# First SwiGLU block: the third of the seven products moved ahead of the second, and the first step of the down projection moved in front of the fourth

## The chip, the cores and the metric

The kernel runs on one core of a Trainium2 chip. The metric is the device time of one execution in microseconds (us). A core has engines that each run their own instructions in order and wait for one another through semaphores: TensorE (PE, with its weight loads shown as PEld), VectorE (DVE), ScalarE (ACT), GpSimd (POOL) and SyncE (SP), which here issues most of the DMA transfers.

## The reference

One decoder layer over 512 tokens of width 1024, in float32. What matters here is its first block, a SwiGLU with a hidden width of 2816 = 22 x 128:

```python
def swiglu(x, w_gate, w_up, w_down):
    return (jax.nn.silu(x @ w_gate) * (x @ w_up)) @ w_down

x = x + 0.5 * swiglu(rms_norm(x, g_ffn1[l]), w_ffn1_gate[l], w_ffn1_up[l], w_ffn1_down[l])
...
x = x + 0.5 * swiglu(rms_norm(x, g_ffn2[l]), w_ffn2_gate[l], w_ffn2_up[l], w_ffn2_down[l])
```

Between the two SwiGLU blocks stand attention over a window, a convolution, attention over a memory, and their output projection; the change does not touch them.

## The kernel before

**Precision.** Every float32 operand of a large product is split into a high and a low part (`whi`, `wlo` for weights; `bh`, `bl` and `hh`, `hl` for activations), and three matmuls (high x high, low x high, high x low) stand for one. ACT makes the high part (L167, a cast), DVE the low part (L168, a subtraction).

**One SwiGLU.** `ffn` goes through the 22 blocks f of 128 hidden columns. Blocks 0 to 3 multiply directly. Blocks 4 to 21 (`fast`, L448) use seven products of half size in place of eight (Strassen's scheme, with the sums of the activations made once by `blocks` and the sums of the weights made for each f by `make_sums`, four additions on DVE, L126 to L129). A product is 12 matmuls of 128x256 (`product`, L439: four slices of the contraction, three matmuls each). In the order of the code before, with the weights that they take, the products are:

| in the code | weights | block of the activations | written to |
|---|---|---|---|
| first | w0, first half (gate) | B_11 | bank `b` |
| second | w0, second half (gate) | B_21 | bank `de`, left half |
| third | w1, first half (sum s12) | B_Q1 | bank `de`, right half |
| fourth | w1, second half (s12) | B_Q2 | bank `b`, added |
| fifth | w2, first half (sum s43) | B_22 | bank `de`, right half, added |
| sixth | w3 (the `vhi`, `vlo` pair) | B_T4 | bank `c` |
| seventh | w2, second half (s43) | B_T3 | bank `b`, added |

After the third product ACT copies the right half of `de` (L459), after the first it copies `b` (L455), after the fourth `b` again (L461). DVE adds `de` and the copies (L464), ACT takes the Silu (L465), and after the sixth and seventh products DVE and ACT finish the hidden block (L475, L479, L402, L403).

**Down projection.** `ROUNDS` cuts the 22 hidden blocks into six rounds. As soon as a round's hidden blocks are there, pieces of its down projection run between later blocks: `steps(f)` gives them, and for f from 8 to 21 there is one piece (`mid`) in each block, two steps `step(j)` of 24 matmuls (in blocks 20 and 21 four of 12), whose sums DVE adds to x (L506). The first step of the piece stands behind the fifth product, the others behind the seventh. A piece has one pair of split weights, d.

**Weights.** `Weights` holds a list of loads (DMAs of 512 KB into four buffers `wraw`) and a list of items, each of which is split into one of four pairs of buffers `whi`, `wlo` in turn, or into the single pair `vhi`, `vlo`. `next()` hands out the item that is next in the list and has the one three places on split (`conv_ahead=3`), so that the order of the items in `add_pair` (L108) has to be that of the calls of `next()` in `fast`, and both decide where the splits stand in the queues of ACT and DVE. Each buffer is free again when the last matmul on what it held is done. The written order is not quite that of the engines: a scheduler of the framework sets it when the program is built, from the dependencies between tiles.

The flag `memory` of `ffn_weights` is true for the first SwiGLU alone, the flag `last` of `ffn` for the second alone. Both SwiGLU blocks run the same `fast` before the change.

Of the kernel before, what the change touches and what calls it, by code (L numbers as in the profile page):

```python
# [34 lines left out]
AF = mybir.ActivationFunctionType  # L35
ALU = mybir.AluOpType
# [49 lines left out]
class Weights:  # L86
# [121 lines left out]
def layer(tc, ctx, a):  # L208
# [185 lines left out]
    def ffn(pool, norm, first, gain, hooks, next_gain, last):  # L394
# [53 lines left out]
        def fast(f, mid):  # L448
# [4 lines left out]
            w0 = W.next()  # L453
            product(b, w0, 0, B_11, True)
            ACT.copy(s12[:, l], b)  # L455
            product(de[:, l], w0, 512, B_21, True)
            w1 = W.next()
            product(de[:, r], w1, 0, B_Q1, True)
            ACT.activation(s45[:, r], de[:, r], AF.Copy, scale=-1.0)  # L459
            product(b, w1, 512, B_Q2, False)  # L460
            ACT.copy(s12[:, r], b)  # L461
            w2 = W.next()
            product(de[:, r], w2, 0, B_22, False)
            DVE.tensor_tensor(g, de, s12, op=ALU.add)  # L464
            ACT.activation(g, g, AF.Silu)  # L465
            rest = []
            for d in mid:
                rest += down(*d)
            if rest:
                rest.pop(0)()  # L470
            w3 = W.next()
            product(c, w3, 0, B_T4, True)
            ACT.copy(s45[:, l], c)
# [759 lines left out]
```

## Time and profile before

| | |
|---|---|
| time, median of three runs | 865.73 us |
| the three runs | 869.84, 865.34, 865.73 us |
| the profiled execution: its time | 870.17 us |
| the profiled execution: its span, first to last instruction | 868.1 us |
| PE busy | 861.3 us (99%) in 6361 matmuls |
| DVE busy | 698.3 us (80%) |
| ACT busy | 446.0 us (51%) |
| transfers | 91.45 MB, 105 GB/s on average |

The page of the profile gives the busy time of each engine over the whole span; its views by window give the same for stretches, a timeline gives each instruction's start and duration, and the view of waits says which engine stood still for which. The first SwiGLU's blocks 4 to 21 lie between about 70 and 340 us of the span, the second's between about 590 and 840 us. A matmul's modelled end lies behind the start of the next, so a busy PE is not PE at its densest: the distance from one start to the next has to be read from the timeline or from counts in windows.

### The profile page before, as it was taken

The numbers are of one execution on the slowest core, as the hardware profiler recorded it, in microseconds if no ns is written. First come the engines' busy times: TensorE is split into PE (matmuls) and PEld (weight loads), VectorE is DVE, ScalarE is ACT, GpSimd is POOL, SyncE is SP. The second block draws the span as 40 slices with busy tenths as digits, with TensorE's granted clock in tenths as the row PEclk, the third lists the DMA queues.
The fourth block names the chain that finished last, engine by engine and source line by source line (L and its number), as shares of the span: only waits on it lengthen the run. The fifth ranks groups of instructions, "written<-read, shape, count | busy, mean of one in ns | idle before, by whom it ended". The sixth has DMA issues, their size and how long they took to land.

```text
span 868.1 us, 15720 instructions
## 1 busy us (share of the span) xinstructions
PE 861.3 (99%) x6361; PEld 795.1 (92%) x6361; DVE 698.3 (80%) x1163; ACT 446.0 (51%) x740; POOL 27.9 (3%) x30
## 2 busy tenths in 40 slices
PE   9999999999999999999999999999999999999998
PEld 5889999999999999988776878889999999999998
DVE  7998877777868887869989976997987878787772
ACT  7455545455554454632939754454554444545440
POOL 0010000000000000300000021010000000000000
PEclk9999999999999999999999999999999999999999
DMA  7326334334454344232020333336333333333312
GB/s 271 122 83 165 94 97 122 99 110 134 111 145 146 97 113 130 95 97 62 0 62 13 110 89 84 99 90 159 105 106 121 95 121 85 116 98 99 121 49 99
DMA packets 34809, 91.45 MB, mean 105 GB/s; under 512 B 3248, under 2 KB 5808, under 8 KB 34736
## 3 DMA queue, kind: packets, MB, share of 16 engines
q1 hardware_dynamic: 32000, 85.99, 32.1%
q0 software_dynamic: 1584, 2.88, 2.1%
q10 hardware_dynamic: 1152, 1.57, 0.7%
q8 instruction: 50, 0.82, 0.4%
q14 instruction: 23, 0.19, 0.1%
HBM read 85.45 MB, written 2.10 MB: 101 GB/s over the span
## 4 chain that ended last, share of the span: by engine, by line
PE 92%; DVE 3%; ACT 2%; issue 1%; DMA 1%; SPq 0%; ACTq 0%; DVEq 0%
PE mm L347 15%; PE mm L348 14%; PE mm L349 14%; PE mm L444 11%; PE mm L446 11%; PE mm L445 11%; PE sc L444 2%; PE sc L446 2%; PE sc L445 2%; PE sc L347 1%; PE sc L349 1%; PE sc L348 1%; PE tp L948 1%; PE tp L962 1%; ACT p L913 1%
## 5 line engine op out<-in xcount | busy, mean ns | idle before, releaser
L444 PE MATMUL mm<-bh,whi 128*128 128x256 f32 x864 | 239.9, 278 | 0.2 <-ACT kept L459 0.2
L446 PE MATMUL mm<-bh,wlo 128*128 128x256 f32 x864 | 239.6, 277 | 0.0
L445 PE MATMUL mm<-bl,whi 128*128 128x256 f32 x864 | 239.6, 277 | 0.0
L348 PE MATMUL mm<-hl,whi 128*128 128x256 f32 (+1 forms) x640 | 184.7, 289 | 0.0
L349 PE MATMUL mm<-hh,wlo 128*128 128x256 f32 (+1 forms) x640 | 184.6, 289 | 0.0
L347 PE MATMUL mm<-hh,whi 128*128 128x256 f32 (+1 forms) x640 | 184.1, 289 | 0.0
L167 ACT CAST whi<-wraw 128x1024 fp32r<-128x1024 f32 (+2 forms) x122 | 124.1, 1021 | 106.2 <-PE mm L348 45.0
L168 DVE TENSOR_TENSOR wlo<-wraw,whi 128x1024 fp32r<-128x1024 f32 (+2 forms) x122 | 145.4, 1193 | 34.4 <-ACT whi L167 34.0
L446 PEld LDWEIGHTS mm<-bh,wlo 128*128 128x128 f32 x864 | 163.1, 189 | 0.0
L444 PEld LDWEIGHTS mm<-bh,whi 128*128 128x128 f32 x864 | 162.2, 188 | 0.5 <-ACT kept L459 0.4
L445 PEld LDWEIGHTS mm<-bl,whi 128*128 128x128 f32 x864 | 162.2, 188 | 0.2
L349 PEld LDWEIGHTS mm<-hh,wlo 128*128 128x128 f32 x640 | 120.8, 189 | 2.9
L347 PEld LDWEIGHTS mm<-hh,whi 128*128 128x128 f32 x640 | 120.1, 188 | 2.7
L348 PEld LDWEIGHTS mm<-hl,whi 128*128 128x128 f32 x640 | 120.1, 188 | 2.7
L168 DVE TENSOR_TENSOR wlo<-s,whi 128x1024 fp32r<-128x1024 f32 x72 | 87.9, 1222 | 36.0 <-ACT whi L167 35.6
L167 ACT CAST whi<-s 128x1024 fp32r<-128x1024 f32 x72 | 75.5, 1050 | 47.3 <-PE mm L445 43.5
L348 PE MATMUL mm<-xl,whi 128*128 128x512 f32 x192 | 75.9, 395 | 0.6 <-DVE xl L359 0.5
L347 PE MATMUL mm<-xh,whi 128*128 128x512 f32 x192 | 76.3, 402 | 0.0
L349 PE MATMUL mm<-xh,wlo 128*128 128x512 f32 x192 | 75.8, 395 | 0.0
L506 DVE SCALAR_TENSOR_TENSOR x<-mm,x 128x512 f32<-128x512 f32 x80 | 54.0, 682 | 3.7 <-PE mm L349 3.7
L167 ACT CAST vhi<-wraw 128x512 fp32r<-128x512 f32 x36 | 22.4, 622 | 62.7 <-PE sc L445 48.5
L126 DVE TENSOR_TENSOR s<-wraw 128x512 f32<-128x512 f32 x36 | 24.9, 691 | 32.6 <-DMA wraw<-in_wgu 32.6
(243 smaller groups left out, 1368.3 us busy)
## 6 DMA issues: line engine op xcount, KB each, us to landing
wraw<-in_wgu SPq DMA_DIRECT2D x86, 512.0 KB, 3.6
wraw<-in_wd SPq DMA_DIRECT2D x44, 512.0 KB, 3.7
wraw<-in_win SPq DMA_DIRECT2D x12, 512.0 KB, 3.5
x<-t POOLq DMA_DIRECT2D x8, 256.0 KB, 6.1
out<-t SPq DMA_DIRECT2D x7, 256.0 KB, 2.0
x<-in_xT SPq DMA_DIRECT2D x3, 512.0 KB, 6.6
wraw<-in_wout_a SPq DMA_DIRECT2D x6, 256.0 KB, 2.7
wraw<-in_wgu SPq DMA_DIRECT2D x4, 256.0 KB, 4.9
```

The source lines that it names most:

```text
L126: nc.vector.tensor_tensor(s12[:, l], u[:, l], u[:, r], op=ALU.add)
L167: nc.scalar.copy(hi[:, :cols], raw[:, :cols])
L168: nc.vector.tensor_tensor(lo[:, :cols], raw[:, :cols], hi[:, :cols].bitcast(F32), op=ALU.subtract)
L347: PE.matmul(ps[:, t], wh[:, w], hi(k)[:, t], start=one, stop=False, skip_group_check=cut > 1)
L348: PE.matmul(ps[:, t], wh[:, w], lo(k)[:, t], start=False, stop=False, skip_group_check=cut > 1)
L349: PE.matmul(ps[:, t], wl[:, w], hi(k)[:, t], start=False, stop=end, skip_group_check=cut > 1)
L444: PE.matmul(ps, wh[:, c], bh[k][:, block], start=one, stop=False, skip_group_check=not first)
L445: PE.matmul(ps, wh[:, c], bl[k][:, block], start=False, stop=False, skip_group_check=not first)
L446: PE.matmul(ps, wl[:, c], bh[k][:, block], start=False, stop=end, skip_group_check=not first)
L506: DVE.scalar_tensor_tensor(o, ps, 0.5, xd, op0=ALU.mult, op1=ALU.add)
L913: ACT.activation(self.p[n, h][:, c], src[h][:, i, c], AF.Exp, scale=self.fac[:, m : m + 1], bias=self.neg[:, m : m + 1], accum_out=self.de ...
L948: PE.transpose(ps[:, i * P : (i + 1) * P], self.p[n, h][:, c : c + P], ident)
```

## The change

In the first SwiGLU alone (`last` false, `memory` true), blocks 4 to 21 take their products in another order, and the list of weights follows:

- the third product (w1, B_Q1, right half of `de`) and ACT's copy of it stand ahead of the second (w0, B_21, left half of `de`), which now adds to a bank that the third has started (`first` is False);
- the first step of the down projection stands ahead of the fourth product, where it stood behind the fifth;
- in `add_pair` the item of the down weights d stands ahead of that of the sum s43.

```diff
-    def add_pair(self, gate, up, mid):
+    def add_pair(self, gate, up, mid, early):
...
         self.items.append((i + 1, 1024, 128, lambda: self.sums[i][0]))
+        if early:
+            for ap in mid:
+                self.add(ap, 128)
         self.items.append((i + 1, 1024, 128, lambda: self.sums[i][1]))
-        for ap in mid:
-            self.add(ap, 128)
+        if not early:
+            for ap in mid:
+                self.add(ap, 128)
...
-                W.add_pair(flat(gu[f, 0]), flat(gu[f, 1]), [down(*d) for d in mid])
+                W.add_pair(flat(gu[f, 0]), flat(gu[f, 1]), [down(*d) for d in mid], memory)
...
+            else:
+                w0 = W.next()
+                product(b, w0, 0, B_11, True)
+                ACT.copy(s12[:, l], b)
+                w1 = W.next()
+                product(de[:, r], w1, 0, B_Q1, True)
+                ACT.activation(s45[:, r], de[:, r], AF.Copy, scale=-1.0)
+                product(de[:, l], w0, 512, B_21, False)
+                rest = []
+                for d in mid:
+                    rest += down(*d)
+                if rest:
+                    rest.pop(0)()
+                product(b, w1, 512, B_Q2, False)
+                ACT.copy(s12[:, r], b)
+                w2 = W.next()
+                product(de[:, r], w2, 0, B_22, False)
+                DVE.tensor_tensor(g, de, s12, op=ALU.add)
+                ACT.activation(g, g, AF.Silu)
```

The lines that are left out before the `else` are the old order under `if last:`. Lines of the changed kernel have other numbers: L459 is L483 there, L168 is L173, L506 is L531, L347 to L349 are L352 to L354, L444 to L446 are L449 to L451.

**PE, block 9, before.** In these rows mm_134 is bank `de` of block 9, mm_133 its bank `b`, whi34 and wlo34 are w1 (s12), whi35 and wlo35 are w2 (s43); a bracket names the engines whose semaphores the instruction waits for. The last row of the third product is followed by the fourth:

```order
L446 MATMUL mm_134_1420<-bh_68_551,wlo34_1327 128x256
L444 MATMUL mm_133_1419<-bh_41_331,whi34_1326 128x256 [waits Activation_49]
L445 MATMUL mm_133_1419<-bl_42_332,whi34_1326 128x256
L446 MATMUL mm_133_1419<-bh_41_331,wlo34_1327 128x256
L444 MATMUL mm_133_1419<-bh_52_389,whi34_1326 128x256
```

Twelve rows on, the fifth product is the first to write bank mm_134 again, and it waits for ACT's copy of the third:

```order
L445 MATMUL mm_133_1419<-bl_69_552,whi34_1326 128x256
L446 MATMUL mm_133_1419<-bh_68_551,wlo34_1327 128x256
L444 MATMUL mm_134_1420<-bh_41_331,whi35_1358 128x256 [waits Activation_49]
L445 MATMUL mm_134_1420<-bl_42_332,whi35_1358 128x256
L446 MATMUL mm_134_1420<-bh_41_331,wlo35_1359 128x256 [waits DVE_49]
```

**PE, block 9, now.** The same place in the changed program, again from the last row of the product with s12; mm_140 is the bank of the down step, whi35 and wlo35 are now its weights d, and whi33 is the gate's w0:

```order
L451 MATMUL mm_134_1422<-bh_68_551,wlo34_1339 128x256
L352 MATMUL mm_140_1480<-hh_91_809,whi35_1358 128x256 [waits DVE_49,Activation_49]
L353 MATMUL mm_140_1480<-hl_92_810,whi35_1358 128x256
L354 MATMUL mm_140_1480<-hh_91_809,wlo35_1359 128x256 [waits DVE_49]
L352 MATMUL mm_140_1480<-hh_101_956,whi35_1358 128x256
L449 MATMUL mm_134_1422<-bh_41_331,whi33_1287 128x256 [waits Activation_49]
L450 MATMUL mm_134_1422<-bl_42_332,whi33_1287 128x256
```

The scheduler has put four matmuls of the down step directly behind the product with s12, and the product that the code names next, B_21 into the left half of the same bank, waits for an instruction of ACT: it is the copy of the right half (L483). The rest of the step follows behind B_21. All of blocks 8 to 21 read so.

**PE, block 6, now.** Blocks 4 to 7 have no down step in that place. Here mm_105 is `de`, mm_104 is `b`, whi21 is w1 and whi20 is w0:

```order
L451 MATMUL mm_105_975<-bh_68_551,wlo21_906 128x256
L449 MATMUL mm_104_974<-bh_41_331,whi21_905 128x256 [waits Activation_49]
L450 MATMUL mm_104_974<-bl_42_332,whi21_905 128x256
L451 MATMUL mm_104_974<-bh_41_331,wlo21_906 128x256
L449 MATMUL mm_104_974<-bh_52_389,whi21_905 128x256
L449 MATMUL mm_105_975<-bh_41_331,whi20_866 128x256 [waits Activation_49]
```

Four matmuls of the product B_Q2 stand there in their stead, and blocks 4 and 7 read the same; in block 5 it is three matmuls of a down step with 512 columns.

**DVE, from block 8 into block 9, before.** wlo35 is the low part of s43 for block 9, wlo36 that of the down weights d, L126 to L129 are the sums for the block after, and mm_129 and mm_132 are the two down steps of block 8:

```order
L126 TENSOR_TENSOR s12_26_1507<-wraw27_1330 128x512 [waits DMAHW4_49]
L129 TENSOR_TENSOR s43_26_1508<-wraw26_1304,wraw27_1330 128x512 [waits DMAHW3_49,DVE_49]
L127 TENSOR_TENSOR s12_26_1507<-wraw26_1304,s12_26_1507 128x512 [waits DVE_49]
L506 SCALAR_TENSOR_TENSOR x_69<-mm_129_1332,x_69 128x512 [waits PE_49]
L128 TENSOR_TENSOR s43_26_1508<-wraw26_1304,s12_26_1507 128x512 [waits DVE_49]
L168 TENSOR_TENSOR vlo37_1458<-wraw24_1181,vhi37_1457 128x512 [waits PE_49,Activation_49]
L475 TENSOR_TENSOR t_128_1238<-kept_126_1236,mm_122_1232 128x512 [waits PE_49,Activation_49]
L479 TENSOR_TENSOR t_128_1238<-t_128_1238,t_127_1237 128x512 [waits DVE_49]
L168 TENSOR_TENSOR wlo35_1359<-s43_23_1321,whi35_1358 128x1024 [waits Activation_49]
L403 TENSOR_TENSOR hl_131_1390<-t_128_1238,hh_130_1389 128x512 [waits Activation_49]
L506 SCALAR_TENSOR_TENSOR x_69<-mm_132_1393,x_69 128x512 [waits PE_49]
L168 TENSOR_TENSOR wlo36_1427<-wraw25_1243,whi36_1426 128x1024 [waits DMAHW2_49,Activation_49]
```

**The same place now**, from the low part of s12 for block 9 (wlo34); wlo36 is here s43, wlo35 the down weights d:

```order
L173 TENSOR_TENSOR wlo34_1339<-s12_23_1332,whi34_1338 128x1024 [waits PE_49,Activation_49]
L494 TENSOR_TENSOR t_127_1239<-mm_123_1235,kept_125_1237 128x512 [waits PE_49,Activation_49]
L131 TENSOR_TENSOR s12_26_1519<-wraw27_1342 128x512 [waits DMAHW4_49,DVE_49]
L134 TENSOR_TENSOR s43_26_1520<-wraw26_1291,wraw27_1342 128x512 [waits DMAHW3_49,DVE_49]
L173 TENSOR_TENSOR vlo37_1446<-wraw24_1181,vhi37_1445 128x512 [waits PE_49,Activation_49]
L500 TENSOR_TENSOR t_128_1240<-kept_126_1238,mm_122_1234 128x512 [waits PE_49,Activation_49]
L132 TENSOR_TENSOR s12_26_1519<-wraw26_1291,s12_26_1519 128x512 [waits DVE_49]
L504 TENSOR_TENSOR t_128_1240<-t_128_1240,t_127_1239 128x512 [waits DVE_49]
L173 TENSOR_TENSOR wlo36_1429<-s43_23_1333,whi36_1428 128x1024 [waits Activation_49]
L408 TENSOR_TENSOR hl_131_1392<-t_128_1240,hh_130_1391 128x512 [waits Activation_49]
L531 SCALAR_TENSOR_TENSOR x_69<-mm_132_1395,x_69 128x512 [waits PE_49]
L173 TENSOR_TENSOR wlo35_1359<-wraw25_1201,whi35_1358 128x1024 [waits DMAHW2_49,Activation_49]
```

The low part of the down weights keeps its place at the end of this run of DVE's work, with one sum (L128, now L133) and one addition to x fewer ahead of it, while the matmul that reads it has moved forward by three products. Blocks 10 to 16, 19 and 20 have these twelve rows too; in 17, 18 and 21 fewer or others stand ahead of the down weights.

More of the change, by code (lines that the diff above doesn't have):

```diff
@@ L452, in fast @@
             s12, s45, g, u = kept(), kept(), work(), work()
[L453 to L470, printed above, removed]
+            if last:
+                w0 = W.next()
+                product(b, w0, 0, B_11, True)
+                ACT.copy(s12[:, l], b)
+                product(de[:, l], w0, 512, B_21, True)
+                w1 = W.next()
[13 more added lines that the diff above has]
+            else:
+                w0 = W.next()
+                product(b, w0, 0, B_11, True)
+                ACT.copy(s12[:, l], b)
+                w1 = W.next()
+                product(de[:, r], w1, 0, B_Q1, True)
+                ACT.activation(s45[:, r], de[:, r], AF.Copy, scale=-1.0)
+                product(de[:, l], w0, 512, B_21, False)
+                rest = []
+                for d in mid:
+                    rest += down(*d)
+                if rest:
+                    rest.pop(0)()
+                product(b, w1, 512, B_Q2, False)
+                ACT.copy(s12[:, r], b)
+                w2 = W.next()
+                product(de[:, r], w2, 0, B_22, False)
+                DVE.tensor_tensor(g, de, s12, op=ALU.add)
+                ACT.activation(g, g, AF.Silu)
             w3 = W.next()
```

## The prediction, made before the changed kernel ran

> **What bounds the kernel now.** I read the page's head first, for the engine that carries the span.
>
> ```profile
> span 868.1 us, 15720 instructions
> PE 861.3 (99%) x6361; PEld 795.1 (92%) x6361; DVE 698.3 (80%) x1163; ACT 446.0 (51%) x740; POOL 27.9 (3%) x30
> PE 92%; DVE 3%; ACT 2%; issue 1%; DMA 1%; SPq 0%; ACTq 0%; DVEq 0%
> ```
>
> PE is busy for 861.3 of 868.1 us and is 92% of the chain that ended last. Time can be won on PE only by filling 6.8 us of idleness or by putting matmuls closer together, and it is lost wherever PE is made to wait. So I compared, in the view by windows, a stretch of each SwiGLU that holds nothing but matmuls of 256 columns:
>
> ```profile
> 150.00:200.00 50.00, 50.00 (x427) 50.00 (x426) 36.53 (x48) 23.59 (x36) 0.00 (x0) 1.00 0.40 121
> 700.00:750.00 50.00, 50.00 (x443) 50.00 (x443) 39.54 (x52) 23.71 (x38) 0.00 (x0) 1.00 0.34 105
> ```
>
> The first numbers after the window are its length, then PE and PEld, busy time and count. Both stretches are 100% busy at a granted clock of 1.00, yet the first SwiGLU does 427 matmuls in 50 us and the second 443. The code is the same. ACT's copy L459 comes once in a block of 132 matmuls and shows the distance in the timeline:
>
> ```profile
> 180.87 0.38 ACT L459 ACTIVATE kept<-mm 128x256 f32<-128x256 f32 x1 [0.50 <-PE mm L446]
> 196.41 0.39 ACT L459 ACTIVATE kept<-mm 128x256 f32<-128x256 f32 x1 [0.50 <-PE mm L446]
> ...
> 652.92 0.38 ACT L459 ACTIVATE kept<-mm 128x256 f32<-128x256 f32 x1 [0.43 <-PE mm L446]
> 667.88 0.38 ACT L459 ACTIVATE kept<-mm 128x256 f32<-128x256 f32 x1 [0.44 <-PE mm L446]
> ```
>
> A block takes 15.54 us in the first SwiGLU and 14.96 us in the second: 117.7 against 113.3 ns from start to start. I call them the slow and the quick pitch. The timeline shows where the slow one begins and ends:
>
> ```profile
> 118.36 1.05 ACT L167 CAST whi<-wraw 128x1024 fp32r<-128x1024 f32 x1
> ...
> 119.29 0.28 PE L446 MATMUL mm<-bh,wlo 128*128 128x256 f32 x1
> 119.31 0.37 ACT L459 ACTIVATE kept<-mm 128x256 f32<-128x256 f32 x1
> ...
> 119.73 0.39 PE L444 MATMUL mm<-bh,whi 128*128 128x256 f32 x1 [0.17 <-ACT kept L459]
> ...
> 119.96 0.28 PE L445 MATMUL mm<-bl,whi 128*128 128x256 f32 x1
> ...
> 276.44 0.28 PE L648 MATMUL mm<-wlo,mh 128*128 128x256 f32 x1
> 276.55 0.28 PE L646 MATMUL mm<-whi,mh 128*128 128x256 f32 x1
> ```
>
> In block 8 the fifth product waited for L459, which stood behind a cast of 1.05 us on ACT. PE's next start was 119.73 in place of 119.29 + 0.11 = 119.40 (0.33 us), and the one after came 0.23 us later instead of 0.11, since the weights of a stopped matmul load only when it is released. From there to 276.55 the pitch is slow: 156 us at 0.58/15.54 is **5.8 us**. It is the only wait of PE in blocks 4 to 21:
>
> ```profile
> PE mm L444 <- ACT kept L459: 0.2, 1, 0.2
> ```
>
> Without the wait (0.44) and the slow pitch the profiled execution of 870.17 us would be **863.9**. The median of the runs, 865.73, lies 4.4 below the profiled one, and one run (869.84) lies beside it, so I take it that the other two had little of the slow pitch; no trace shows them. 0.5%, about what a measurement of this kernel can tell from no change, is 4.3 us: 861.4 to 870.1.
>
> **The change, part by part.** No work is added or removed; 18 blocks are reordered.
>
> *Block 8's wait.* The intended cover is there: the fifth product now has B_21, a down step and B_Q2 between itself and the copy it waits for. That wait goes: -0.44.
>
> *A new wait.* B_21 now writes the left half of the bank whose right half ACT is copying, and the built order has B_21's first row wait for that copy, four matmuls behind the third product. What the copy takes is in the timeline of an undisturbed block:
>
> ```profile
> 652.55 0.28 PE L446 MATMUL mm<-bh,wlo 128*128 128x256 f32 x1
> ...
> 652.67 0.28 PE L444 MATMUL mm<-bh,whi 128*128 128x256 f32 x1
> ```
>
> The third product's last matmul starts at 652.55 and gives way at 652.67. The copy (row above) runs from 652.92 to 653.30, 0.63 us after that. With 0.05 us from the copy's end to PE's start (119.68 to 119.73 in block 8), B_21 can start 0.68 us behind the third product; four matmuls cover 0.45. So PE waits 0.23, plus 0.11 for the late weights: **0.34 us**. Bounds: 0.23 if the weights load in time, and 1.4 where ACT is late as in block 8. ACT is idle ahead of the copy otherwise (0.43 in the row), so I take 0.34. Block 5 has three matmuls of 512 columns there and no wait. In block 8 the cast still stands ahead of the copy: it ended at 119.68, the third product gave way at 119.29 - 11 x 0.113 = 118.04, so 1.64 + 0.05 - 0.45 + 0.11 = 1.35 (bounds 0.34 and 1.35; the same late cast is likeliest).
>
> A sentence of the Trainium skill bears on this wait. The row is that of 119.73: there PE writes the bank again 0.05 us after ACT has left it, though it was the same half. The page "PSUM — Partial Sum Buffer", section "Terms", states that two engines on one bank and the same partitions at once is a collision with wrong data, whichever columns they use. By that rule the wait is needed and the sum keeps its 17 waits; if only columns counted, it would lose all of them. No row here shows PE in the other half of a bank that ACT reads, so the trace does not test it; the bracket in the built order is what I go by.
>
> *The down weights.* The step's third matmul needs `wlo` of d. It is the last of twelve instructions that DVE now runs without a gap, from the low part of s12 on. Before, the same run, in the second SwiGLU at the quick pitch:
>
> ```profile
> 698.91 0.28 PE L444 MATMUL mm<-bh,whi 128*128 128x256 f32 x1
> ...
> 700.07 1.23 DVE L168 TENSOR_TENSOR wlo<-s,whi 128x1024 fp32r<-128x1024 f32 x1 [1.45 <-ACT whi L167]
> 701.22 0.68 DVE L464 TENSOR_TENSOR t<-mm,kept 128x512 f32<-128x512 f32 x1
> 702.47 0.69 DVE L126 TENSOR_TENSOR s<-wraw 128x512 f32<-128x512 f32 x1 [0.57 <-DMA wraw<-in_wgu]
> 703.08 0.69 DVE L129 TENSOR_TENSOR s<-wraw,wraw 128x512 f32<-128x512 f32 x1
> 703.68 0.69 DVE L127 TENSOR_TENSOR s<-wraw,s 128x512 f32<-128x512 f32 x1
> ...
> 707.41 1.22 DVE L168 TENSOR_TENSOR wlo<-s,whi 128x1024 fp32r<-128x1024 f32 x1
> 708.54 0.68 DVE L403 TENSOR_TENSOR hl<-t,hh 128x512 fp32r<-128x512 f32 x1
> 709.14 0.68 DVE L506 SCALAR_TENSOR_TENSOR x<-mm,x 128x512 f32<-128x512 f32 x1
> 709.75 1.21 DVE L168 TENSOR_TENSOR wlo<-wraw,whi 128x1024 fp32r<-128x1024 f32 x1
> ```
>
> Here 698.91 is where B_Q2 ended (its buffers come free) and the run starts 1.16 us later. From start to start an instruction of 1024 columns takes 1.14 us and one of 512 takes 0.60. Of the twelve, two of 1024 and nine of 512 stand ahead of the last: 2.28 + 5.40, and 1.22 for the last itself, 8.90. So `wlo` is there 1.16 + 8.90 = 10.06 us after B_Q2's end and PE sees it at 10.11. Up to that matmul PE has B_22, T4, T3 (36), the second down step (24), the next block's B_11 and B_Q1 (24) and two of the step: 86 at 113.3 ns, 9.75 us. Before, three more products stood between, 4.1 us of cover; that cover is gone. PE waits 0.36 + 0.11 = **0.47 us**, and what is queued behind is B_21, whose own wait is then over (it comes 0.23 + 0.47 + 0.23 behind the third product). Nothing else waits behind, as DVE's next instruction is a sum for the block after. This holds for blocks 9 to 16 and 20; block 19 has 0.4 us more PE work in between (the four transposes at 297.54, quoted below), in 17, 18 and 21 DVE has less ahead. Bounds: nothing if DVE gains 0.4 us, 1.0 if the 0.57 us for the transfer in the row stays. I take 0.47, without the transfer: the next `up` is now loaded some 4 us behind `gate` instead of close to it,
>
> ```profile
> DMA to landing us min/median/max: 3.4/3.6/4.4
> ```
>
> and at 3.6 us it lands about when DVE comes to it. The other splits, Silu, and SP's queue keep their order and have microseconds of room.
>
> *The sum.* Copy's wait in blocks 4, 6, 7, 17, 18, 19, 21: 7 x 0.34 = 2.4. Down weights: 9 x 0.47 = 4.2. Block 8: 1.35. Together 8.0 on 863.9 is **871.9** at the quick pitch.
>
> *The slow pitch.* Each of the 17 stops is of the kind that began it. Besides 119.73, the trace has two restarts of such matmuls:
>
> ```profile
> 282.46 0.37 PE L444 MATMUL mm<-bh,whi 128*128 128x256 f32 x1
> 282.67 0.28 PE L445 MATMUL mm<-bl,whi 128*128 128x256 f32 x1
> 282.79 0.28 PE L446 MATMUL mm<-bh,wlo 128*128 128x256 f32 x1
> ...
> 283.03 0.28 PE L445 MATMUL mm<-bl,whi 128*128 128x256 f32 x1
> 283.14 0.28 PE L446 MATMUL mm<-bh,wlo 128*128 128x256 f32 x1
> ...
> 297.54 0.60 PE L678 MATMUL tp<-ident,t 128*128 128x128 f32 x4
> 297.89 0.36 PE L444 MATMUL mm<-bh,whi 128*128 128x256 f32 x1
> ...
> 298.68 0.28 PE L444 MATMUL mm<-bh,whi 128*128 128x256 f32 x1
> 298.79 0.28 PE L445 MATMUL mm<-bl,whi 128*128 128x256 f32 x1
> ```
>
> both behind small matmuls, and both back from 0.12 us and more to 0.11 us within 0.8 us. One of three stayed slow. Blocks 4 to 21 hold 18 x 84 + 14 x 48 = 2184 matmuls; all slow would cost 2184 x 4.4 ns = 9.6, less 9 x 0.13, as 86 matmuls then take 10.12 us and the wait for the down weights shrinks to the copy's: +8.4. Bounds 0 and 8.4; a third is 2.8. **871.9 + 2.8 = 874.7.**
>
> **The rivals.**
> - *Slow throughout.* The first stop locks the slow pitch and no later one releases it: 871.9 + 8.4 = 880.3. For it: it held over 156 us and across small matmuls. Against: a stop in each block is a new start, and two of three returned.
> - *Not slower.* The change removes block 8's late wait and with it the slow pitch (5.8 + 0.44), at block 8; the new waits are only the copy's. It decides if DVE has `wlo` of d within 9.75 us of B_Q2 and the short stops restart cleanly. Then 863.9 + 17 x 0.23 to 17 x 0.34: 867.8 to 869.7, no change by 0.5%. For it: the margin is only 0.36 us in a run of 10. Against: every duration in that run repeats within 0.02 us in the rows.
> - *Late transfers.* DVE's sum waits 0.5 us for `up` in nine blocks as in the row at 702.47: +4.5, 876 to 880.
> - *No stops.* The copy ends within four matmuls, or the built waits cost nothing: 863.9. Against it stand the 0.63 us of the copy's row and the bracket in the built order. The change would then do what it says; as built, B_21 cuts the down step in two.
>
> **How the numbers follow.** Forecast with waits as summed and up to two thirds slow (871.9 to 877.5): 0.65. Slow throughout: 0.14. Not slower: 0.13. Late transfers: 0.05. No stops: 0.03, of which 0.01 for a time under 861.4. Slower by over 0.5% (above 870.1): 0.65 + 0.14 + 0.05 = 0.84; within 0.5%: 0.15; faster: 0.01. The likeliest is the forecast, 874.7. The range leaves out "no stops" and the extremes: 867.8 at "not slower" to 881.0 at "slow throughout" with some transfers late.
>
> **What would show it.** In the profile after, PE should wait for ACT's copy L483 in about eight blocks and for DVE's L173 (`wlo`) in about nine, with 0.2 to 0.4 us each and none for L459's kind at the fifth product; the windows of the first SwiGLU should count 427 to 443 matmuls per 50 us less the stops. The prediction is wrong if PE has no waits there, if the waits for `wlo` are missing (DVE quicker than summed), or if the windows show the quick pitch through all stops or the slow one through all.

## The result, and the profile after

| | before | after |
|---|---|---|
| median, runs | 867.91 us, 8 runs (864.48 to 872.75) | 876.41 us, 8 runs (874.64 to 877.31) |
| ratio, 95% interval | | 1.0098, 1.0068 to 1.0127 |
| profiled execution: time, span | 870.17, 868.1 us | 877.31, 875.1 us |

The change makes the kernel slower by 1%, 876.4 us where 874.7 was predicted. The runs of before fall into two groups, 864.5 to 866.0 and 869.8 to 872.8; those of after do not. Against the faster group of before, after is 10 to 11 us slower by its median. The head of after's page:

```profile
span 875.1 us, 15729 instructions
PE 865.9 (99%) x6361; PEld 796.7 (91%) x6361; DVE 696.5 (80%) x1163; ACT 444.4 (51%) x740; POOL 27.8 (3%) x30
PE 87%; DVE 6%; issue 2%; ACT 2%; DMA 2%; SPq 0%; DVEq 0%; ACTq 0%
```

PE's share of the chain fell from 92 to 87%, and DVE's rose from 3 to 6%: work on DVE now lies on that chain in places. The waits of PE's weight loads say where (engine, line and tile that waited, what for, us in total, times, longest). In after, L449 is a product's first matmul, L354 the third of each three of the down projection, L173 `wlo`, L483 the copy of the third product.

```profile
PEld mm L449 <- ACT kept L483: 3.3, 12, 0.7
PEld mm L354 <- DVE wlo L173: 2.0, 5, 0.4
```

PE's own row of waits shows only the tail of a stop, since a matmul's modelled end (0.28 us) lies behind the start of the next (0.11); its weight loads show nearly all of it. Both waits that the prediction named are there, and the old one, of the fifth product for the copy, is gone. The timeline of block 7 shows the copy's wait:

```profile
109.31 0.28 PE L451 MATMUL mm<-bh,wlo 128*128 128x256 f32 x1
109.34 0.39 ACT L483 ACTIVATE kept<-mm 128x256 f32<-128x256 f32 x1 [1.05 <-PE mm L451]
109.42 0.74 PE L449 MATMUL mm<-bh,whi 128*128 128x256 f32 x2
109.77 0.19 PEld L449 LDWEIGHTS mm<-bh,whi 128*128 128x128 f32 x1 [0.28 <-ACT kept L483]
110.00 0.28 PE L450 MATMUL mm<-bl,whi 128*128 128x256 f32 x1
```

The copy ends at 109.73. B_21's first matmul, the second of the two in the merged row, has its weights loaded from 109.77 and starts with them; the matmul behind it follows at 110.00, 0.22 us later instead of 0.11. Together 0.24 + 0.11 us. The wait for the down weights, in block 13:

```profile
197.17 1.22 DVE L173 TENSOR_TENSOR wlo<-wraw,whi 128x1024 fp32r<-128x1024 f32 x1
...
197.95 0.28 PE L353 MATMUL mm<-hl,whi 128*128 128x256 f32 x1
...
198.45 0.19 PEld L354 LDWEIGHTS mm<-hh,wlo 128*128 128x128 f32 x1 [0.42 <-DVE wlo L173]
198.45 0.39 PE L354 MATMUL mm<-hh,wlo 128*128 128x256 f32 x1 [0.22 <-DVE wlo L173]
...
198.67 0.28 PE L352 MATMUL mm<-hh,whi 128*128 128x256 f32 x1
```

From 197.95 the next start is 0.50 us away instead of 0.11, and the one behind it 0.22: 0.38 + 0.11. So much for stops. The windows of blocks without a stop inside show the pitch (length, then busy time and count of PE and PEld):

```profile
121.00:135.00 14.00, 14.00 (x121) 14.00 (x120) 10.59 (x16) 6.78 (x10) 0.00 (x0) 1.00 0.27 81
137.00:151.00 14.00, 14.00 (x126) 14.00 (x125) 10.24 (x14) 6.74 (x10) 0.00 (x0) 1.00 0.38 114
152.00:166.00 14.00, 14.00 (x121) 14.00 (x120) 9.78 (x14) 6.59 (x10) 0.00 (x0) 1.00 0.37 114
```

121 matmuls in 14 us is the slow pitch, 126 the quick one (both counts include matmuls that reach over an edge of the window). It was slow without a break from block 8 on before; now it changes from block to block, at a granted clock of 1.00 throughout.

**The account.** From the starts of all pairs of neighbouring matmuls of 256 columns with 128x128 weights I summed two things: stops (a distance over 0.127 us, what lies above 0.1133) and the slow pitch (0.115 to 0.127 us, what lies above 0.1133). The two bounds are my choice. Before: 0.8 us of stops and 6.0 of slow pitch in a span of 868.1. After: 7.3 and 6.1 in 875.1. Span less both is 861.3 before and 861.7 after. So 6.5 of the 7.0 us between the two executions are the stops, and the slow pitch cost the same in both, in other places.

### The profile page after: what moved, and what is told of

Its sections match the earlier page's. It is cut to its first block, busy times and chain, and to the rows that moved or that the text cites. A ratio compares the mean times of both kernels' runs of the same rounds, so it can differ in the third digit from the quotient of the medians.

```text
span 875.1 us, 15729 instructions
## 1 busy us (share of the span) xinstructions
PE 865.9 (99%) x6361; PEld 796.7 (91%) x6361; DVE 696.5 (80%) x1163; ACT 444.4 (51%) x740; POOL 27.8 (3%) x30
## 4 chain that ended last, share of the span: by engine, by line
PE 87%; DVE 6%; issue 2%; ACT 2%; DMA 2%; SPq 0%; DVEq 0%; ACTq 0%
PE mm L354 15%; PE mm L352 15%; PE mm L353 15%; PE mm L449 10%; PE mm L450 10%; PE mm L451 10%; DVE wlo L173 2%; PE sc L450 2%; PE sc L449 2%; PE sc L451 2%; PE sc L352 1%; PE sc L354 1%; PE sc L353 1%; PE tp L973 1%; DMA wraw<-in_wgu 1%
## 5 line engine op out<-in xcount | busy, mean ns | idle before, releaser
L449 PE MATMUL mm<-bh,whi 128*128 128x256 f32 x864 | 241.2, 279 | 1.0 <-ACT kept L483 0.5
L451 PE MATMUL mm<-bh,wlo 128*128 128x256 f32 x864 | 239.5, 277 | 0.0
L173 DVE TENSOR_TENSOR wlo<-wraw,whi 128x1024 fp32r<-128x1024 f32 (+2 forms) x122 | 145.6, 1194 | 52.9 <-ACT whi L172 52.4
L354 PE MATMUL mm<-hh,wlo 128*128 128x256 f32 (+1 forms) x640 | 185.6, 291 | 1.0 <-DVE wlo L173 0.9
L352 PE MATMUL mm<-hh,whi 128*128 128x256 f32 (+1 forms) x640 | 184.1, 289 | 0.0
L449 PEld LDWEIGHTS mm<-bh,whi 128*128 128x128 f32 x864 | 162.6, 188 | 3.7 <-ACT kept L483 3.3
L451 PEld LDWEIGHTS mm<-bh,wlo 128*128 128x128 f32 x864 | 162.4, 188 | 0.0
L354 PEld LDWEIGHTS mm<-hh,wlo 128*128 128x128 f32 x640 | 120.2, 188 | 5.1 <-DVE wlo L173 2.0
L173 DVE TENSOR_TENSOR wlo<-s,whi 128x1024 fp32r<-128x1024 f32 x72 | 87.9, 1222 | 45.9 <-ACT whi L172 45.8
L352 PEld LDWEIGHTS mm<-hh,whi 128*128 128x128 f32 x640 | 120.6, 188 | 2.7
L352 PE MATMUL mm<-xh,whi 128*128 128x512 f32 x192 | 76.2, 401 | 0.6 <-ACT xh L363 0.6
L354 PE MATMUL mm<-xh,wlo 128*128 128x512 f32 x192 | 75.9, 396 | 0.0
L531 DVE SCALAR_TENSOR_TENSOR x<-mm,x 128x512 f32<-128x512 f32 x80 | 54.3, 685 | 2.0 <-PE mm L354 1.6
L352 PEld LDWEIGHTS mm<-xh,whi 128*128 128x128 f32 x192 | 36.1, 189 | 12.1 <-issue 2.0
```

Of the source, the lines that this page charges most:

```text
L173: nc.vector.tensor_tensor(lo[:, :cols], raw[:, :cols], hi[:, :cols].bitcast(F32), op=ALU.subtract)
L352: PE.matmul(ps[:, t], wh[:, w], hi(k)[:, t], start=one, stop=False, skip_group_check=cut > 1)
L354: PE.matmul(ps[:, t], wl[:, w], hi(k)[:, t], start=False, stop=end, skip_group_check=cut > 1)
L449: PE.matmul(ps, wh[:, c], bh[k][:, block], start=one, stop=False, skip_group_check=not first)
L451: PE.matmul(ps, wl[:, c], bh[k][:, block], start=False, stop=end, skip_group_check=not first)
L531: DVE.scalar_tensor_tensor(o, ps, 0.5, xd, op0=ALU.mult, op1=ALU.add)
```

## The experiments

All twelve profiled executions close in the same way: span less stops less slow pitch is 861.2 to 862.7 us. The runs of before beside the experiments had medians of 866.25 (first four, 28 runs), 865.85 (e5 to e8, 27) and 865.62 us (e9, e10, 18).

| run | median us (lowest to highest, runs) | ratio to before, 95% | stops, us | slow pitch, us |
|---|---|---|---|---|
| e1 products alone | 873.34 (871.91 to 874.26, 9) | 1.0077, 1.0054 to 1.0101 | 6.8 | 3.1 |
| e2 step alone | 869.82 (867.95 to 871.81, 12) | 1.0033, 1.0008 to 1.0059 | 0.3 | 6.0 |
| e3 B_21 in its own bank | 865.06 (864.08 to 872.98, 12) | 1.0002, 0.9969 to 1.0034 | 0.3 | 7.7 |
| e4 in both SwiGLUs | 886.93 (884.94 to 889.24, 4) | 1.0236, 1.0193 to 1.0280 | 15.8 | 5.5 |
| e5 own bank, step first | 869.32 (867.18 to 872.37, 10) | 1.0030, 1.0002 to 1.0059 | 3.2 | 1.7 |
| e6 more work on DVE | 876.44 (875.25 to 877.25, 4) | 1.0114, 1.0075 to 1.0153 | 7.6 | 5.2 |
| e7 step behind B_Q2 | 872.34 (870.77 to 875.12, 10) | 1.0066, 1.0041 to 1.0092 | 8.1 | 2.4 |
| e8 products, own bank | 865.01 (864.26 to 866.19, 12) | 0.9984, 0.9965 to 1.0003 | 0.3 | 1.1 |
| e9 B_21 between | 873.67 (873.34 to 876.93, 5) | 1.0090, 1.0057 to 1.0123 | 6.5 | 3.1 |
| e10 one stop | 866.95 (865.57 to 874.35, 12) | 1.0016, 0.9985 to 1.0047 | 0.9 | 2.7 |

Stops and slow pitch are of the one profiled execution. My theory: two new waits, for the copy because two halves share a bank, and for `wlo` because PE has too little work ahead of it; each stop may also start the slow pitch. The rival: the order itself is the cause (late transfers, other buffers), or the stops cost nothing.

### The parts of the change alone (e1, e2)

e1 keeps the change's order of products and puts step and list back; e2 is before with the step and the list of the change:

```diff
 e1, against after:
                 product(de[:, l], w0, 512, B_21, False)
-                rest = []
-                for d in mid:
-                    rest += down(*d)
-                if rest:
-                    rest.pop(0)()
                 product(b, w1, 512, B_Q2, False)
 e2, against before:
                 ACT.activation(s45[:, r], de[:, r], AF.Copy, scale=-1.0)
+                rest = []
+                for d in mid:
+                    rest += down(*d)
+                if rest:
+                    rest.pop(0)()
                 product(b, w1, 512, B_Q2, False)
```

> Only the third product moved ahead of the second; the first step of the down projection and its weights are back behind the fifth. Theory (PE waits for ACT's copy of the same bank in each block, and each stop may start the slow pitch): 17 waits of 0.34 us and one of 1.3 us in block 8, no wait for the down weights, together 7 us on 864, and the slow pitch in about half of the blocks, 4 to 6 us: 874 to 877 us, nearly the time of the full change. Rival (the loss comes from the down weights that are asked for early): no stops to speak of, 864 to 867.

> Only the down step moved in front of the fourth product, its weights listed early; the second and third products in the old order. Theory: B_21 writes the bank ahead of the copy, so no product waits for the copy, and the down weights have one product (1.36 us) more of cover than in the change, more than the 0.36 us that they were late: at most one stop, the stop of block 8 is gone too, under 100 matmuls at the slow pitch, 864 to 866 us in every run. Rival (the early step is what costs): nine waits of 0.3 us or more for the split of the down weights, 868 to 874.

The weight loads' waits of e1:

```profile
PEld mm L449 <- ACT kept L483: 4.6, 15, 0.9
```

e1 has the copy's wait and no other, as expected; it gives 6.8 us of stops, and its slow pitch was half of after's, so that the time is a little under what I expected. e2 came out 4 us later than expected, at a time that lies in the range of its rival (868 to 874). But the rival's nine waits are not there, and neither of the two waits is; what there is, the timeline shows in block 8:

```profile
118.23 0.69 DVE L408 TENSOR_TENSOR hl<-t,hh 128x512 fp32r<-128x512 f32 x1
...
118.97 0.19 PEld L353 LDWEIGHTS mm<-hl,whi 128*128 128x128 f32 x1
119.01 0.35 PE L353 MATMUL mm<-hl,whi 128*128 128x256 f32 x1
...
119.19 0.28 PE L354 MATMUL mm<-hh,wlo 128*128 128x256 f32 x1
```

DVE has block 7's `h_lo` ready at 118.92, just when the down step, now earlier, comes to it. The load ahead of that matmul follows at 118.97 and the next start is at 119.19, 0.07 us late. From there the distance is 0.12 us, and 1322 matmuls up to 276.0 keep it: 6.0 us of slow pitch behind a stop of 0.07.

### The bank (e3, e8)

e3 is the full change, e8 is e1, each with B_21 in a bank of its own, so that it need not wait for the copy of its neighbour; DVE then adds in two halves:

```diff
-                product(de[:, l], w0, 512, B_21, False)
+                e = sc_bank()[:, l]
+                product(e, w0, 512, B_21, True)
...
-                DVE.tensor_tensor(g, de, s12, op=ALU.add)
+                DVE.tensor_tensor(g[:, l], e, s12[:, l], op=ALU.add)
+                DVE.tensor_tensor(g[:, r], de[:, r], s12[:, r], op=ALU.add)
```

> The full change, but B_21 goes to a bank of its own (from the pool of two banks that the sixth product uses), and DVE adds the two halves in two instructions of 256 columns. Theory: with no shared bank there is no wait for the copy; the scheduler then has no reason to put four matmuls of the step ahead of B_21, so that B_21 covers the late down weights too: no stops, no slow pitch, 864 to 866 us. Rival (the new order costs by itself, by its weights or its place among DVE's work): 870 or more as in the change.

> The order of the products alone, as in the run of the products alone, with B_21 in a bank of its own. If the shared bank is all that the order of the products costs, the 6.8 us of stops go and the time is that of before: 864 to 866, with a second group at 870 to 873 where the slow pitch starts; no stop in blocks 4 to 21, and none in block 8, since two products stand between the copy and the fifth product. Rival: the third product so early is waited for by something else (weights of w1, buffers): stops stay, 868 to 873 in one group.

No stop is left in blocks 4 to 21 of either. The windows of e3, then of e8:

```profile
72.00:84.00 12.00, 12.00 (x104) 12.00 (x104) 9.90 (x15) 6.94 (x12) 0.00 (x0) 1.00 0.51 152
```

```profile
72.00:84.00 12.00, 12.00 (x108) 12.00 (x107) 10.05 (x15) 6.74 (x13) 0.00 (x0) 1.00 0.38 107
```

PE is busy all the time in both. e8 against e1 shows it cleanest (the addition in two halves and a later choice of the sixth product's bank, which the edit also needs, put no stop there): the same order of products, 6.8 us of stops with the shared bank and none without, 873.3 against 865.0 us. In e3 the built order has all of B_21 ahead of the step once it waits for nothing, so the down weights have twelve matmuls more of cover, and that wait goes too. "No slow pitch" in its expectation missed: e3's profiled execution was at the slow pitch from its first fast block, with no stop ahead of it: 104 matmuls in 12 us where e8 has 108. Its runs show both pitches, seven at 864.1 to 865.6 and five at 871.6 to 873.0.

e8 is the best version found: all twelve runs lie at 864.3 to 866.2, while 6 of the 27 runs of before beside it lie at 870.1 to 872.2. Its median is not told apart from that of before (0.9965 to 1.0003). That it has no slower group is not shown: e10, whose code differs in block 8 alone, was at the slow pitch before that block.

### Twice as much of the change (e4)

The change in the second SwiGLU as well (`early` true, and the new branch taken for `last` too):

```diff
-            if last:
+            if False:
```

> The change made in the second SwiGLU as well. Theory: the same stops there, about 12 of 0.47, 5 of 0.34 and one larger, 8 to 9 us, and the slow pitch that the second SwiGLU never had before, in about half of its blocks, 4 to 7 us: 876.4 plus 12 to 16, 888 to 892 us. Rival (stops and slow pitch belong to the first SwiGLU's surroundings): under 880, with the second SwiGLU at the quick pitch of 443 matmuls per 50 us.

```profile
PEld mm L354 <- DVE wlo L173: 6.6, 15, 0.6
PEld mm L449 <- ACT kept L483: 5.8, 21, 0.9
```

The two waits go from 2.0 and 3.3 us in after to 6.6 and 5.8, the stops from 7.3 to 15.8 us and the time rises by another 10.5. The two waits belong to the order, wherever it is used. The slow pitch did not grow with them (5.5 us in the profiled execution, the fastest of the four), which is why the time is a little under the expectation.

### The down weights' cover (e5, e6, e9)

e5 takes the copy's wait away and keeps the step ahead of B_21; e6 computes `h_lo` twice, e9 half of `wlo` of the down weights twice:

```diff
 e5, against e3:
-                e = sc_bank()[:, l]
-                product(e, w0, 512, B_21, True)
                 rest = []
...
+                e = sc_bank()[:, l]
+                product(e, w0, 512, B_21, True)
 e6, against after:
             DVE.tensor_tensor(h_lo[f], t, h_hi[f].bitcast(F32), op=ALU.subtract)
+            if not last and f >= 8:
+                DVE.tensor_tensor(h_lo[f], t, h_hi[f].bitcast(F32), op=ALU.subtract)
 e9, against after:
                 nc.vector.tensor_tensor(lo[:, :cols], raw[:, :cols], hi[:, :cols].bitcast(F32), op=ALU.subtract)
+                if i in self.mids:
+                    nc.vector.tensor_tensor(lo[:, :512], raw[:, :512], hi[:, :512].bitcast(F32), op=ALU.subtract)
```

> The full change, B_21 in a bank of its own (its sum with s12 in two halves), and the down step written ahead of B_21, so that its third matmul stands again 86 matmuls behind B_Q2's end. This takes the wait for ACT's copy away and leaves the wait for the down weights. If the cover of 9.75 us against DVE's 10.1 us is what makes PE wait there, the trace shows no wait for L483 and waits for wlo of the down weights of 0.3 to 0.5 us plus 0.11 in those of blocks 9 to 16 and 20 that are entered at the quick pitch, next to none in blocks at the slow pitch (10.12 us of cover); with one longer stop of about 1 us in block 8, where the weights come late (they were there at 120.05 in the run with the step alone). Stops 3 to 6 us, 869 to 875. Rival: the wait for the down weights was a consequence of the copy's wait (PE held up by ACT, then DVE's buffers free later): no stops, 864 to 866, or 870 to 873 with the slow pitch.

> The full change, with DVE's h_lo of blocks 8 and later of the first SwiGLU computed twice: one more instruction of 512 columns (0.60 us from start to start) in the run that ends with wlo of the down weights. If DVE's run is what PE waits for, the waits for wlo grow by 0.60 in the blocks entered at the quick pitch (0.36 to about 0.95) and appear with 0.5 to 0.6 in those at the slow pitch, in blocks 9 to 16 and 20, and the copy's wait is then hidden there: +4.5 to +6 us on 876.4, 881 to 883. Rival: the wait is set by a transfer or by ACT's cast, and DVE's time lies beside it: 876 to 877.

> The full change, with half of wlo of the down weights computed twice on DVE (0.60 us more ahead of the matmul that waits for it). As built, the matmuls then stand in another order: the step gives way to B_21 after its second matmul instead of its fourth, and two of B_Q2 fill the place, so that B_21's twelve matmuls (1.36 us) lie between the second and the third of the step. If the wait for wlo is a matter of cover (9.75 against 10.1 us), it goes in spite of the longer work on DVE (about 11.3 against 10.7 us), and the copy's wait, no longer hidden behind it, comes in every block: 16 times 0.24 + 0.11 and block 8 about 1: 6 to 7 us of stops and none for wlo in blocks 9 to 16, 873 to 876. Rival: wlo is waited for whenever DVE works longer: its waits grow by 0.6 in nine blocks, 880 to 883.

e6 did not do what it was for. As built, the second `h_lo` (L410) stands behind `wlo` of the down weights; the timeline of DVE:

```profile
196.94 1.23 DVE L173 TENSOR_TENSOR wlo<-wraw,whi 128x1024 fp32r<-128x1024 f32 x1
198.07 0.70 DVE L410 TENSOR_TENSOR hl<-t,hh 128x512 fp32r<-128x512 f32 x1
```

So 0.6 us more per block on DVE costs nothing there: 876.44 beside 876.41. But in its block 9 a transfer did by chance what the edit was to do:

```profile
125.95 1.22 DVE L173 TENSOR_TENSOR wlo<-s,whi 128x1024 fp32r<-128x1024 f32 x1 [1.64 <-ACT whi L172]
...
128.28 0.69 DVE L131 TENSOR_TENSOR s<-wraw 128x512 f32<-128x512 f32 x1 [0.51 <-DMA wraw<-in_wgu]
...
134.24 1.22 DVE L173 TENSOR_TENSOR wlo<-wraw,whi 128x1024 fp32r<-128x1024 f32 x1
```

DVE's run from the low part of s12 to the end of `wlo` took 9.50 us there, 0.6 more than the 8.91 of block 13 in after, and PE, come at the quick pitch, waited 0.98 us in place of 0.38.

e5 missed in the place that mattered. The copy's wait is gone and block 8 has a long stop (1.45 us), though not for the weights: the step, now earlier still, waits for block 7's `h_hi` and `h_lo`,

```profile
119.42 0.39 PE L353 MATMUL mm<-hl,whi 128*128 128x256 f32 x1 [0.70 <-DVE hl L408]
```

but `wlo` is waited for only at 208.89 (block 14) and 327.90 (block 21); the other blocks pass without such a wait. DVE's timeline tells why, ahead of the step of block 13 in after and of block 12 in e5:

```profile
189.49 1.23 DVE L173 TENSOR_TENSOR wlo<-s,whi 128x1024 fp32r<-128x1024 f32 x1 [1.64 <-ACT whi L172]
...
191.23 0.69 DVE L131 TENSOR_TENSOR s<-wraw 128x512 f32<-128x512 f32 x1
191.83 0.69 DVE L134 TENSOR_TENSOR s<-wraw,wraw 128x512 f32<-128x512 f32 x1
...
193.63 0.69 DVE L132 TENSOR_TENSOR s<-wraw,s 128x512 f32<-128x512 f32 x1
...
197.17 1.22 DVE L173 TENSOR_TENSOR wlo<-wraw,whi 128x1024 fp32r<-128x1024 f32 x1
198.31 0.69 DVE L133 TENSOR_TENSOR s<-wraw,s 128x512 f32<-128x512 f32 x1
```

```profile
169.91 1.23 DVE L173 TENSOR_TENSOR wlo<-s,whi 128x1024 fp32r<-128x1024 f32 x1
...
174.16 0.69 DVE L131 TENSOR_TENSOR s<-wraw 128x512 f32<-128x512 f32 x1
...
177.10 1.22 DVE L173 TENSOR_TENSOR wlo<-wraw,whi 128x1024 fp32r<-128x1024 f32 x1
...
178.84 0.68 DVE L132 TENSOR_TENSOR s<-wraw,s 128x512 f32<-128x512 f32 x1
179.43 0.68 DVE L134 TENSOR_TENSOR s<-wraw,wraw 128x512 f32<-128x512 f32 x1
180.04 0.68 DVE L133 TENSOR_TENSOR s<-wraw,s 128x512 f32<-128x512 f32 x1
```

Three of the four additions for the block after stand ahead of `wlo` in after, one in e5, and an addition to x (L531, here L534) has gone behind it too. DVE then waits 1.48 us for ACT's `vhi` in e5, so that the run gets shorter by 0.5 us only, 8.41 in place of 8.91. That is enough: `wlo` ends at 178.32, just ahead of its matmul at 178.49. I had taken DVE's order as given in the expectation. Block 14 of e5 decides between the count of cover and its rival, by which the wait was a consequence of the copy's: there is no wait for the copy, but the addition to x stands ahead of `wlo` again, and PE waits 0.49 us.

```profile
206.42 0.69 DVE L534 SCALAR_TENSOR_TENSOR x<-mm,x 128x512 f32<-128x512 f32 x1
...
207.62 1.22 DVE L173 TENSOR_TENSOR wlo<-wraw,whi 128x1024 fp32r<-128x1024 f32 x1
```

The prediction's count can be redone for blocks 9 to 16 from the starts in the traces: DVE's run begins 1.16 or 1.17 us behind B_Q2's end, PE sees its end 0.05 us later, and the 86 matmuls are the cover. What is left over is the wait (without the 0.11 us for the late weights):

| run, block | DVE's run, us | cover, us | wait by the count | wait measured |
|---|---|---|---|---|
| after, 13 | 8.91 | 9.75 (quick) | 0.38 | 0.38 |
| after, 11 | 8.90 | 10.12 (slow) | none | none |
| after, 9, a transfer 0.22 us late | 9.22 | 10.12 (slow) | 0.32 | 0.31 |
| e6, 9, a transfer 0.51 us late | 9.50 | 9.75 (quick) | 0.97 | 0.98 |
| e5, 12 | 8.41 | 9.75 (quick) | none | none |
| e5, 14, an addition to x more | 9.01 | 9.75 (quick) | 0.48 | 0.49 |

e9 tests the cover from the other side. `wlo` is longer by 0.6 us, but B_21's twelve matmuls now stand ahead of the one that needs it. The weight loads' waits of e9 (its lines are four higher):

```profile
PEld mm L453 <- ACT kept L487: 4.5, 17, 0.3
PEld mm L358 <- DVE wlo L177: 0.5, 1, 0.5
```

One wait for `wlo` in place of five (in block 21), and the copy's in seventeen blocks; the time, 873.67, is in the expected range, though block 8's stop is 0.34 us and not about 1. With more work on DVE and still more cover there is no wait: what counts is DVE's run less PE's cover, not how long DVE works. It shows too that the two waits are not a sum: where the copy's was hidden behind the other, it comes back when the other goes (6.5 us of stops in e9, 7.3 in after).

### Another place for the step (e7)

The step of e2, moved behind B_Q2:

```diff
-                rest = []
-                for d in mid:
-                    rest += down(*d)
-                if rest:
-                    rest.pop(0)()
                 product(b, w1, 512, B_Q2, False)
                 ACT.copy(s12[:, r], b)
+                rest = []
+                for d in mid:
+                    rest += down(*d)
+                if rest:
+                    rest.pop(0)()
```

> The step of the down projection alone, as in the run of the step alone, but behind B_Q2 instead of ahead of it: 12 matmuls (1.36 us) more cover for wlo of the down weights, and the third product's copy has B_Q2 and a step ahead of the product that waits for it. No stop at all expected in blocks 4 to 21. If a stop, however short, is what starts the slow pitch (0.07 us did so in the run of the step alone), it stays quick: 863 to 865 in all runs. If the slow pitch starts without a stop, runs lie in two groups, 863 to 866 and 870 to 873, as those of before.

Missed: there are eight new stops of 0.35 to 2.2 us, seven of them of one kind. The weight loads' waits, and DVE's row ahead of the longest one:

```profile
PEld mm L449 <- ACT kept L480: 6.7, 7, 2.2
```

```profile
205.55 0.69 DVE L131 TENSOR_TENSOR s<-wraw 128x512 f32<-128x512 f32 x1 [4.17 <-DMA wraw<-in_wgu]
```

B_Q2 waits for the copy of the first product, which stands on ACT behind casts. In eight blocks in a row a sum on DVE waited 2.4 to 4.6 us for a transfer, and ACT waits for DVE behind it. The length of the stop does not follow from that alone: the same 4.17 us stand ahead of the shortest of the seven (0.35) and the longest (2.19), ahead of which ACT also has work of the attention over the memory to do (L619, L631, L625). So e7 is in part the rival of late transfers, by its own order; no run shows how much of its stops they are. On the pitch it shows that a stop need not start the slow one: behind six of the eight it is quick.

### One stop in a kernel without stops (e10)

```diff
 against e8:
-                e = sc_bank()[:, l]
-                product(e, w0, 512, B_21, True)
+                e = de[:, l] if f == 8 else sc_bank()[:, l]
+                product(e, w0, 512, B_21, f != 8)
```

> The order of the products alone with B_21 in a bank of its own in all blocks but block 8, where it shares the bank again and waits for the late copy (0.87 + 0.11 us in the run of the products alone). One stop, everything else as in the run without stops, which lay at 864.3 to 866.2 in all twelve runs. If a single stop can start the slow pitch and nothing ends it before the memory's products at about 270 us, some or all runs lie 6 us above the others: a group at 865 to 867 (the stop alone, +1) and one at 870.5 to 873. Rival: the pitch is drawn anew for some other reason, and the stop costs its 1 us: all runs at 865 to 867.5.

Nine runs lie at 865.6 to 867.9 and three at 872.0 to 874.4. The profiled one, 867.87, shows something else than I had written: the windows before and after block 8, and the stop itself.

```profile
100.00:110.00 10.00, 10.00 (x87) 10.00 (x86) 8.29 (x12) 6.21 (x11) 0.00 (x0) 1.00 0.29 99
121.00:135.00 14.00, 14.00 (x126) 14.00 (x125) 11.11 (x16) 6.57 (x12) 0.00 (x0) 1.00 0.29 99
```

```profile
118.28 0.28 PE L449 MATMUL mm<-bh,whi 128*128 128x256 f32 x1
118.87 0.38 PE L449 MATMUL mm<-bh,whi 128*128 128x256 f32 x1 [0.31 <-ACT kept L483]
119.09 0.29 PE L450 MATMUL mm<-bl,whi 128*128 128x256 f32 x1
```

It was slow from the first fast block (69.94, no stop ahead of it), and the one stop ended it: 87 matmuls in 10 us before, 126 in 14 us behind. So a stop can change the pitch in both directions. The group at 872 and above fits runs in which the slow pitch stayed or came behind the stop; no trace shows one of them.

## Why the prediction was right, and where its sizes were off

**Base, 863.9.** Right: e8, without a stop in blocks 4 to 21 and with 1.1 us of slow pitch, took 864.90 in its profiled execution.

**The copy's wait, 0.34 in each of seven blocks, 2.4.** Right in size: 0.34 to 0.35 in blocks 4, 6, 7, 17, 19 and 21, 0.29 in 18, and 0.11 in block 5, where none was counted: 2.5. That the shared bank is its cause is shown by e1 against e8.

**The down weights, 0.47 in nine blocks, 4.2.** The mechanism is right, the sum 3.7. In four blocks entered at the quick pitch it is 0.49 or 0.50. Block 9 was entered at the slow pitch and stopped for 0.42 all the same, since a transfer was 0.22 us late there (table above). In blocks 11, 14, 16 and 20 PE came to `wlo` at the slow pitch and waited for it no more than the late weights; the copy's wait took its place, 0.28 to 0.36 in all. The prediction had this shrinking, but only in its bound. So PE waited for `wlo` in five blocks and for the copy in twelve, where about nine and about eight were forecast.

**Block 8, 1.35.** 0.78. The cast L167 was no longer what stood ahead of the copy; it was `h_hi`'s, which in turn waited for DVE. DVE had worked without a gap since 112.88, where a sum had waited 1.86 us for a transfer; whether the stop would be gone without that, no run shows. The timeline of ACT and PE:

```profile
119.48 0.62 ACT L407 CAST hh<-t 128x512 fp32r<-128x512 f32 x1 [0.97 <-DVE t L504]
120.01 0.38 ACT L483 ACTIVATE kept<-mm 128x256 f32<-128x256 f32 x1
120.44 0.39 PE L449 MATMUL mm<-bh,whi 128*128 128x256 f32 x1 [0.51 <-ACT kept L483]
```

Together the stops are 7.0 in place of 8.0.

**The slow pitch, one third, 2.8.** This is the term that was mis-sized: 6.1 us. Behind the stops of 9 of the 18 blocks it was slow, and in block 5 it became slow at 87.91, behind matmuls of 512 columns, where I had taken one restart in three from three restarts in the trace of before. That a later stop can release the slow pitch was right and decided against the rival "slow throughout"; the share was not to be had from three cases. Nor is it one number: behind the 18 stops of e1 the pitch was slow 3 times, behind those of e9 5 times. In after it changed behind 15 of the 18, in e1 behind 6, in e9 behind 3. Over all twelve traces it was slow behind 37 of 121 stops of 0.1 us and more: a third was near the mean, but this order did not keep to it, and why is open. The account is then 870.17 - 0.44 - 6.0 + 7.0 + 6.1 = 876.8 for the profiled 877.31. The two errors, -1.0 and +3.3, partly cancel; that the forecast is 1.7 us off is partly luck.

**Rivals.** "Not slower" needed DVE in time: five blocks show it was not. "Late transfers", 0.5 us in nine blocks, did not occur at that size: of the nine blocks only block 9 has one, of 0.22 us (L131 at 128.95). Elsewhere the additions for the next block follow the instruction ahead of them without a gap (191.23 and 191.83, no releaser in the rows). "No stops" is what e3 and e8 make of it.

The sentence of the Trainium skill on banks ("PSUM — Partial Sum Buffer", "Terms") stands untested: in no run did PE write one half of a bank while ACT read the other. The sum went by the built order, which kept the two apart, and giving B_21 its own bank took the wait away.

## What to carry to other kernels

Moving work forward on a saturated engine moves it toward the operands that it waits for: before it is moved, count for each operand how much work remains between its release and its use, and look for tiles that share a bank with what another engine still reads. Two such waits at one place are not a sum: with one gone the other appears. And when a count leaves a margin smaller than one instruction (0.36 us here against 0.60), the scheduler's order decides it, so that the built order has to be read again for every variant.

## What the runs showed of the hardware that was not expected

In these traces, matmuls of 256 columns run at one of two pitches, 113.3 or 117.8 ns from start to start, at the same granted clock (1.00 in the windows) and with weight loads that show the same 0.19 us. A pitch holds for hundreds of matmuls: some 1700 in e3. The slow one can start without any wait, on the change from matmuls of 512 to 256 columns (e3, e10, block 5 of after), and behind stops of 0.05 us (e8, at 338.10) to 0.98 us (block 9 of e6). One stop can also end it (e10).

At one place it is the same in all twelve executions, whatever the pitch before: the 48 matmuls of the memory's first product (`mm<-mh,whi` and its two companions, at 270.46 to 276.08 in before) run at 117.8 ns from the third on, behind small matmuls and a stop of 0.09 us, and of the 48 behind them, which take the same two kinds of operands with their roles exchanged (`mm<-whi,mh`, from 276.19), those from the seventh on run at 113.3 ns, without a stop. That is where the long slow stretches of before, e2 and e3 ended. So it is not chance alone, and the operands or where they lie are a candidate.

Worth up to 7.7 us in an execution, the pitch would explain most of the 8.9 us between the runs of e3, a kernel without stops in blocks 4 to 21; none of its quicker runs was traced. What sets the pitch is open: no run changed the addresses of the tiles or the phase of a restart alone.
